# A two-layer fp32 encoder on one core: exchanges issued by GpSimd, later rotary steps, an output projection in two parts, and a last chunk finished block by block

## The chip, the cores and the metric

The kernel runs on one core of one Trainium2 chip. The metric is the device time of one execution in microseconds (us). Three runs of the kernel before gave 2165.27, 2164.92 and 2161.17 us, median 2164.92. The engines are TensorE (PE, matrix multiplications; PEld is its weight load), VectorE (DVE), ScalarE (ACT), GpSimd (POOL) and SyncE (SP, which computes nothing and issues DMAs).

## The reference, cut to what matters

```python
for l in range(2):                                   # 256 tokens, D = 2048, float32
    h = rms(x, ln1_g[l]);  proj = h @ w_in[l]         # 12 column groups: A, B and C heads
    # A: 4 heads, low-rank q and kv, q = rms(a_cq) @ w_uq, kv = rms(a_ckv) @ w_ukv, rotary on 64 columns
    # B: 6 query heads, 2 kv heads, RMSNorm on q and k, 2-D axial rotary
    # C: 6 heads, rotary, mixture of three dilated windows weighted by their log-sum-exp
    mixed = concat([rms(o_a), rms(o_b), rms(o_c)]) * g_out[l]
    x = x + mixed @ w_out[l]                          # output projection, 2048 x 2048
    u = square(relu(rms(x, ln2_g[l]) @ w_ff1[l]))     # 2048 x 8192
    x = x + u @ w_ff2[l]                              # 8192 x 2048
return rms(x, ln_f_g)
```

## The kernel before

Every product is an emulated fp32 one. A weight chunk of 1024 columns (`raw`) is copied by ACT into a rounded part `hi` (L157), and DVE forms `lo = raw - hi` (L158); activations are split in the same way, and TensorE multiplies hi by hi, hi by lo and lo by hi. All weights of the two layers stream once from HBM through three `raw` tiles of 2048 columns, loaded by SP (L142), into five chunk buffers of `hi` and `lo`.

The work is a list of units (L50 to L62), one per weight tile: s0 to s3 and a4 to a7 (low-rank inputs), b0 to b7 with un, ur, uk, uv between (A's and B's queries and keys), v0 to v7 (values), c0 to c11 (two units for each head of C), o0 to o9, w0 to w5 and p0 to p7 (output projection), then f0 to f63 and g0 to g63 (MLP, in four rounds of 16 f and 16 g). A unit of o or w is one chunk of 1024 columns with 12 matmuls; the others are two chunks. A loop (L1042 to L1053) runs a slot for each unit: its matmuls, the functions scheduled at "pre", one split of a chunk, "mid", splits up to five chunks ahead, "post", the eviction of the unit, and "ext". What is scheduled where is written with `at(unit, place, function, offset in units)`; each engine executes its instructions in the order of this program.

A projected pair of q and k (tile `z`, evicted from PSUM by L263) needs its partition halves exchanged for the rotary step: `swap` (L337 to L342) copies them by DMA into `zs`, four DMAs of 64 KB for the B group and two of 128 KB for C. SP issues them (L340, L341), in one queue with the weight loads. `rope` (L348) then multiplies both tiles, L355 adds them, and L360 and L361 split the result into the ring tiles of the score matmuls. The heads table (L837) says for each head in which unit the scores (`s_mm`) stand, two units later the transposes, three later the product with the values (`pv_mm`, L737 to L739).

The output projection's 16 k-tiles are the 4 of A, the 6 of B and the 6 of C. Units o0 to o9 do the ten tiles of A and B for column chunks 0 and 1, w0 to w5 C's six for the same chunks, and p0 to p7 all sixteen for chunks 2 and 3; `add_out` (L877) adds a chunk to the residual stream `xt` and takes its squares. f0 (L922) is special: after its first ten k-tiles come the transposes of chunk 3 of the new residual (L278), whose operands (L201 on ACT, L202 on DVE) its own last k-tiles read. The end (L1056 to L1065) starts when the last g unit is done for both blocks of 128 tokens: squares, their mean, a power on GpSimd (L232), then scaling and storing of both blocks.

## Time and profile before

| what | value |
|---|---|
| median of three runs | 2164.92 us |
| the profiled execution: time | 2162.03 us |
| the profiled execution: span of the trace | 2160.0 us |
| busy share of PE, DVE, ACT, POOL | 99%, 63%, 48%, 4% |
| HBM traffic over the span | 183 GB/s |
| DMA queue of SP and ACT | 53.2% of 16 engines' span |
| exchanges: DMAs of 64 KB and 128 KB | 40 and 24 |

Times in the trace count from the start of the span. A row of the timeline gives start and duration, the engine, the program line and the tiles, and in brackets how long the engine had stood idle before it and whose work ended that. A busy share is a mean over the whole span: TensorE is nearly always busy, so the rows to look for are the few at which it stands still, and the stretches in which its granted clock is lower.

### The profile page before, as it was taken

What the parts mean: (1) busy time and instruction counts of PE and PEld (TensorE: products, weight loads), DVE (VectorE), ACT (ScalarE), POOL (GpSimd) and SP (SyncE); (2) the same over time, 40 slices, a digit from 0 to 9 for tenths busy, and PEclk for the clock granted to TensorE, in tenths of its full rate; (3) what the DMA queues carried; (4) which work ended last, traced back from release to release, by engine and by line L of the source; (5) the groups of instructions that cost most, each with busy time, mean ns of one, the idle gap of its engine ahead of it and who ended that gap; (6) DMA issues with size and microseconds to landing.
All of it is one profiled execution on the core that took longest, in us unless ns stands there. A gap on an engine that the chain in (4) does not pass through costs nothing.

```text
span 2160.0 us, 27992 instructions
## 1 busy us (share of the span) xinstructions
PE 2132.9 (99%) x11132; PEld 1825.8 (85%) x11132; DVE 1367.7 (63%) x1867; ACT 1037.8 (48%) x1549; POOL 90.8 (4%) x108
## 2 busy tenths in 40 slices
PE   9999999999999999999999999999999999999997
PEld 8888878888888888888888888788888888888886
DVE  7787865665564565566577778656646655655654
ACT  7555554543453444344454565545434434534443
POOL 2001110000000000000020011100000000000000
PEclk9999999999999999999999999999999999999999
DMA  8644454555555555555554544545655555565563
GB/s 303 202 154 147 151 193 163 195 195 201 174 206 199 175 190 203 177 191 191 199 185 166 170 149 154 196 159 195 211 195 176 199 194 175 193 214 176 187 223 117
DMA packets 64018, 401.90 MB, mean 186 GB/s; under 512 B 7824, under 2 KB 7824, under 8 KB 19216
## 3 DMA queue, kind: packets, MB, share of 16 engines
q1 hardware_dynamic: 61440, 394.29, 53.2%
q10 hardware_dynamic: 2448, 5.83, 0.8%
q8 instruction: 87, 1.43, 0.3%
q14 instruction: 43, 0.35, 0.0%
HBM read 392.23 MB, written 2.10 MB: 183 GB/s over the span
## 4 chain that ended last, share of the span: by engine, by line
PE 56%; issue 37%; DVE 3%; ACT 2%; DMA 1%; POOL 0%; SPq 0%; POOLq 0%; DVEq 0%; ACTq 0%
PE acc L307 16%; PE acc L639 8%; PE acc L641 8%; PE acc L640 8%; PE acc L308 8%; PE acc L416 1%; PE att L307 1%; DMA z<-z 1%; DVE lo L158 1%; PE att L737 1%; ACT hi L157 1%; PE acc L417 1%; DVE z L348 1%; PE att L738 1%; PE att L739 1%
## 5 line engine op out<-in xcount | busy, mean ns | idle before, releaser
L158 DVE TENSOR_TENSOR lo<-raw,hi 128x1024 fp32r<-128x1024 f32 (+1 forms) x735 | 883.2, 1228 | 377.9 <-ACT hi L157 373.5
L307 PE MATMUL acc<-hx,hi 128*128 128x512 f32 x2720 | 950.4, 394 | 1.7 <-ACT hi L157 1.7
L157 ACT ACTIVATE hi<-raw 128x1024 fp32r<-128x1024 f32 (+1 forms) x735 | 752.7, 1051 | 380.1 <-PE acc L641 348.0
L308 PE MATMUL acc<-hx,lo 128*128 128x256 f32 x2720 | 761.6, 280 | 1.5 <-DVE lo L158 1.5
L307 PEld LDWEIGHTS acc<-hx,hi 128*128 128x128 f32 x2720 | 512.5, 188 | 114.9 <-ACT hi L157 2.4
L308 PEld LDWEIGHTS acc<-hx,lo 128*128 128x128 f32 x2720 | 511.8, 188 | 2.4 <-DVE lo L158 2.1
L639 PE MATMUL acc<-hi,ring 128*128 128x512 f32 x1296 | 506.7, 391 | 0.0
L641 PE MATMUL acc<-hi,ring 128*128 128x512 f32 x1296 | 504.8, 389 | 0.0
L640 PE MATMUL acc<-lo,ring 128*128 128x512 f32 x1296 | 504.7, 389 | 0.0
L641 PEld LDWEIGHTS acc<-hi,ring 128*128 128x128 f32 x1296 | 243.5, 188 | 51.0
L639 PEld LDWEIGHTS acc<-hi,ring 128*128 128x128 f32 x1296 | 243.6, 188 | 50.0
L640 PEld LDWEIGHTS acc<-lo,ring 128*128 128x128 f32 x1296 | 243.7, 188 | 49.7
L262 ACT ACTIVATE t<-acc 128x256 f32<-128x256 f32 x192 | 73.4, 384 | 310.1 <-PE acc L308 304.3
L263 DVE TENSOR_TENSOR t<-acc,t 128x256 f32<-128x256 f32 x140 | 59.1, 424 | 123.2 <-ACT t L262 123.2
L943 ACT ACTIVATE ring<-t 128x256 fp32r<-128x256 f32 x128 | 53.5, 418 | 126.0 <-DVE t L941 126.0
L972 DVE SCALAR_TENSOR_TENSOR xt<-acc,st,xt 128x512 f32<-128x512 f32 x64 | 45.8, 751 | 86.2 <-PE acc L641 86.2
L944 DVE TENSOR_TENSOR ring<-t,ring 128x256 fp32r<-128x256 f32 x128 | 54.4, 425 | 62.6 <-ACT ring L943 62.6
L267 ACT ACTIVATE sq<-xt 128x512 f32<-128x512 f32 x40 | 25.1, 629 | 71.7 <-DVE xt L972 44.0
L941 DVE SCALAR_TENSOR_TENSOR t<-t 128x256 f32<-128x256 f32 x128 | 54.4, 425 | 4.4
L639 PE MATMUL acc<-hi,hx 128*128 128x512 f32 x128 | 50.9, 398 | 0.0
L640 PE MATMUL acc<-lo,hx 128*128 128x512 f32 x128 | 50.0, 391 | 0.0
L641 PE MATMUL acc<-hi,hx 128*128 128x512 f32 x128 | 49.9, 390 | 0.0
(152 smaller groups left out, 1273.5 us busy)
## 6 DMA issues: line engine op xcount, KB each, us to landing
raw<-in_w_dram SPq DMA_DIRECT2D x347, 1024.0 KB, 4.9
raw<-in_w_dram SPq DMA_DIRECT2D x39, 512.0 KB, 3.7
z<-z SPq DMA_DIRECT2D x24, 128.0 KB, 3.7
z<-z SPq DMA_DIRECT2D x40, 64.0 KB, 4.2
ring<-in_xfeat_dram SPq DMA_DIRECT2D x8, 256.0 KB, 7.5
ring<-in_tabs_dram ACTq DMA_DIRECT2D x8, 256.0 KB, 4.6
xt<-in_xtok_dram ACTq DMA_DIRECT2D x2, 1024.0 KB, 10.0
ring<-in_gfin_dram ACTq DMA_DIRECT2D x4, 256.0 KB, 4.3
```

The lines of the kernel that those rows point to most:

```text
L157: act.activation(out=hi[:, :n], in_=t, func=AF.Copy)
L158: dve.tensor_tensor(out=lo[:, :n], in0=t, in1=hi[:, :n].bitcast(F32), op=ALU.subtract)
L262: act.activation(out=t, in_=acc[:, T:], func=AF.Copy)
L263: dve.tensor_tensor(out=dst, in0=acc[:, :T], in1=t, op=ALU.add)
L307: pe.matmul(acc, h, s, start=k == 0, stop=False)
L308: pe.matmul(acc[:, T:], lo, s[:, :T], start=False, stop=k == n - 1)
L639: pe.matmul(a, sh, h, start=first, stop=False)
L640: pe.matmul(a, sh, lo, start=False, stop=False)
L641: pe.matmul(a, sl, h, start=False, stop=last)
L941: dve.scalar_tensor_tensor(out=z, in0=z, scalar=0.0, in1=z, op0=ALU.max, op1=ALU.mult)
L943: act.activation(out=d[:, :T], in_=z, func=AF.Copy)
L944: dve.tensor_tensor(out=d[:, T:], in0=z, in1=d[:, :T].bitcast(F32), op=ALU.subtract)
```

## The change

- The exchanges of `swap` are issued from GpSimd's queue and no longer from SP's.
- The first weight unit is split into four chunks of 512 columns, and its second half is loaded as two DMAs.
- B's rotary multiplication (`b_rope`) moves from "post" of its u unit to "pre" of the unit after it; the last C head's rotary step moves one more unit back, and C's last three heads get their transposes and value products one or two units later.
- o0 to o19 now do A's and B's ten k-tiles for all four column chunks, w0 to w11 C's six; the p units are gone. Each chunk is added to the residual twice; its squares are taken at the second time. C's group sum moves from o6 to o9.
- f0 does its first 12 k-tiles and then the transposes of chunk 3; f1 does its own first 12, then the last four of f0 and of itself. Both are evicted in f1's slot.
- In the last layer the last two g units run all of block 0 first and then all of block 1, and `last_chunk` finishes and stores each block by itself.

```diff
--- before
+++ after
...
 def split_chunks(u, n):
     if u == 0:
-        return [512, 512, 1024]
+        return [512] * 4
     return [n] if n <= 1024 else [n // 2, n // 2]
...
     names += [f"c{m}" for m in range(12)]
-    names += [f"o{m}" for m in range(10)]
-    names += [f"w{m}" for m in range(6)]
-    names += [f"p{m}" for m in range(8)]
+    names += [f"o{m}" for m in range(20)]
+    names += [f"w{m}" for m in range(12)]
     for q in range(4):
...
     xf = [ring() for _ in range(8)]
-    parts = [(0, 0, 512), (0, 512, 1024), (0, 1024, 2048), (1, 0, 1024), (1, 1024, 2048), (2, 0, 1024),
-             (2, 1024, 2048)]
+    parts = [(0, 0, 512), (0, 512, 1024), (0, 1024, 1536), (0, 1536, 2048), (1, 0, 1024), (1, 1024, 2048),
+             (2, 0, 1024), (2, 1024, 2048)]
     for g in range(8):
         sp.dma_start(out=xf[g], in_=xfeat[g])
-        if g == 0:
-            load_part(*parts.pop(0))
-        if parts:
-            load_part(*parts.pop(0))
+        for _ in range(2 if g < 2 else 1):
+            if parts:
+                load_part(*parts.pop(0))
     loaded[0] = RAW_BUFS
...
             for a in range(0, P, 2 * w):
-                sp.dma_start(out=zs[a:a + w], in_=z[a + w:a + 2 * w])
-                sp.dma_start(out=zs[a + w:a + 2 * w], in_=z[a:a + w])
+                pool.dma_start(out=zs[a:a + w], in_=z[a + w:a + 2 * w])
+                pool.dma_start(out=zs[a + w:a + 2 * w], in_=z[a:a + w])
             return z, zs
...
             at(name, "pre", b_sq)
-            at(name, "post", lambda p=p: b_rope(p))
+            at(name, "pre", lambda p=p: b_rope(p), 1)
             at(name, "pre", lambda p=p: b_rope2(p), 2)
...
-        def v_mm(name, srcs, k0, kt, accs=None, n=4):
-            for k in range(n):
+        def v_mm(name, srcs, k0, kt, accs=None, n=4, blocks=(0, 1)):
+            for k, tb in [(k, tb) for k in range(n) for tb in blocks]:
                 h, lo = wtile(base + POS[name], k, 512)
...
                 first, last = k0 + k == 0, k0 + k == kt - 1
...
+                a = (accs or st["accv"])[tb]
+                sh = s[:, tb * P:(tb + 1) * P]
+                sl = s[:, T + tb * P:T + (tb + 1) * P]
+                pe.matmul(a, sh, h, start=first, stop=False)
+                pe.matmul(a, sh, lo, start=False, stop=False)
+                pe.matmul(a, sl, h, start=False, stop=last)
...
         for h in range(6):
-            d = 1 if h == 5 else 0
+            d = 2 if h == 5 else 0
             at(POS["c0"] + 2 * h + 2 + d, "pre" if d else "post", lambda h=h: c_rope(h))
...
-        heads = [("A", h, POS["b7"] + h) for h in range(4)]
-        heads += [("B", h, POS["v2"] + h) for h in range(6)]
-        heads += [("C", h, POS["c3"] + 2 * h + (h == 5)) for h in range(6)]
-        for (g, h, s) in heads:
+        heads = [("A", h, POS["b7"] + h, 2, 3) for h in range(4)]
+        heads += [("B", h, POS["v2"] + h, 2, 3) for h in range(6)]
+        heads += [("C", h, POS["c3"] + 2 * h, 2, 3) for h in range(3)]
+        heads += [("C", 3, POS["c9"], 2, 4), ("C", 4, POS["c11"], 3, 5), ("C", 5, POS["o3"], 3, 5)]
+        for (g, h, s, dt, dp) in heads:
             hs = {}
-            at(s + 3, "ext", lambda g=g, h=h, hs=hs: pv_mm(g, h, hs))
-            at(s + 2, "ext", lambda hs=hs: transp(hs))
+            at(s + dp, "ext", lambda g=g, h=h, hs=hs: pv_mm(g, h, hs))
+            at(s + dt, "ext", lambda hs=hs: transp(hs))
             at(s, "ext", lambda g=g, h=h, hs=hs: s_mm(g, h, hs))
-            at(s + 4, "pre", lambda g=g, h=h, hs=hs: o_ev(g, h, hs))
-            at(s + 3, "pre", lambda hs=hs: t_copy(hs))
+            at(s + dp + 1, "pre", lambda g=g, h=h, hs=hs: o_ev(g, h, hs))
+            at(s + dt + 1, "pre", lambda hs=hs: t_copy(hs))
             at(s + 1, "pre", lambda g=g, h=h, hs=hs: s_max(g, h, hs))
...
-        for (g, name, n, k0, per) in (("A", "v5", 4, 0, 2), ("B", "c3", 6, 4, 2), ("C", "o6", 6, 10, 3)):
+        for (g, name, n, k0, per) in (("A", "v5", 4, 0, 2), ("B", "c3", 6, 4, 2), ("C", "o9", 6, 10, 1)):
             s = POS[name]
...
             at(s + 1, "pre", lambda g=g, n=n: grp_fin(g, n * P))
-            d = 1 if g == "B" else 0
+            d = 0 if g == "A" else 1
             at(s + 1 + d, "pre" if d else "post", diag("r" + g))
...
-        def add_out(accs, c):
+        def add_out(accs, c, whole):
             for tb in range(2):
                 dve.tensor_tensor(out=xc(tb, c), in0=accs[tb], in1=xc(tb, c), op=ALU.add)
-            for tb in range(2):
-                square_sum(st2["ssx"], tb, c)
+            if whole:
+                for tb in range(2):
+                    square_sum(st2["ssx"], tb, c)
...
+        def mk_o(name, c, j, k0, n):
             def f():
...
                     st["acco", c] = [accbank(), accbank()]
...
+                mixed = [st["mixed"].get(k0 + k) for k in range(2 * n)]
+                v_mm(name, mixed, 2 * j, 2 * n, st["acco", c], 2)
+            define(name, f, lambda: add_out(st["acco", c], c, k0 > 0) if j == n - 1 else None)
+            if k0 and j == n - 1 and c < 3:
+                turn(name, 1, c)
+        for i in range(20):
+            mk_o(f"o{i}", i // 5, i % 5, 0, 5)
+        for i in range(12):
+            mk_o(f"w{i}", i // 3, i % 3, 10, 3)
...
+            def part(i, ks):
+                if ks[0] == 0:
+                    st2["acc", i] = accbank()
+                acc = st2["acc", i]
+                for k in ks:
+                    h, lo = wtile(base + POS[f"f{i}"], k)
+                    s = st2["hx"][k]
+                    pe.matmul(acc, h, s, start=k == 0, stop=False)
+                    pe.matmul(acc[:, T:], lo, s[:, :T], start=False, stop=k == KT - 1)
             def f():
                 if i == 0:
...
+                    part(0, range(12))
+                    st2["turn"] = x_transposes(3)
+                elif i == 1:
+                    part(1, range(12))
+                    part(0, range(12, KT))
+                    part(1, range(12, KT))
+                else:
+                    st2["acc", m] = gemm_acc(f"f{i}", 0, st2["hx"])
+            def evict():
+                if i == 1:
+                    ev(0)
+                if i:
+                    ev(m)
+            def ev(m):
                 acc = st2.pop(("acc", m))
...
+        at("f0", "post", lambda: x_operands(3, st2["turn"], st2, G_LN2, l))
         at("f2", "post", r2_fin)
...
                     st["accg"] = [accbank(), accbank()]
+                if l + 1 == DEPTH and i >= 62:
+                    v_mm(f"g{i}", st2["u"], 4 * j, 16, st["accg"], blocks=(0,))
+                    if i == 63:
+                        for d in (1, 0):
+                            v_mm(f"g{i - d}", st2["u"], 4 * (j - d), 16, st["accg"], blocks=(1,))
+                    return
                 v_mm(f"g{i}", st2["u"], 4 * j, 16, st["accg"])
...
                 if j < 3:
+                    return
+                if i == 63 and l + 1 == DEPTH:
+                    last_chunk(st["accg"], st["r2sq"])
                     return
...
             at("g48", "post", load_gfin)
+            at("g62", "post", first_means)
...
             dve.tensor_tensor(out=xc(tb, c), in0=xc(tb, c), in1=gf[c], op=ALU.mult)
+    def first_means():
+        for tb in range(2):
+            t = stat(2)
+            dve.tensor_reduce(out=t[:, 0:1], in_=final_state["ssx"][:, 4 * tb:4 * tb + 3], axis=AX.X, op=ALU.add)
+            dve.tensor_scalar(out=t[:, 1:2], in0=t[:, 0:1], scalar1=1.0 / D, scalar2=EPS, op0=ALU.mult, op1=ALU.add)
+            final_state["mean", tb] = t[:, 1:2]
+    def last_chunk(accs, scale):
+        ss = final_state["ssx"]
+        y = [ring() for _ in range(2)]
+        for tb in range(2):
+            dve.scalar_tensor_tensor(out=xc(tb, 3), in0=accs[tb], scalar=scale[:, tb:tb + 1], in1=xc(tb, 3),
+                                     op0=ALU.mult, op1=ALU.add)
+            square_sum(ss, tb, 3)
+            dve.tensor_tensor(out=y[tb], in0=xc(tb, 3), in1=gf[3], op=ALU.mult)
+            ms, r = stat(2), stat(2)
+            dve.tensor_scalar(out=ms[:, 0:1], in0=ss[:, 4 * tb + 3:4 * tb + 4], scalar1=1.0 / D,
+                              scalar2=final_state["mean", tb], op0=ALU.mult, op1=ALU.add)
+            pool.tensor_tensor(out=r[:, 0:1], in0=ms[:, 0:1], in1=nhalf[:, 0:1], op=ALU.pow)
+            dve.tensor_scalar(out=xt[tb][:, :1024], in0=xt[tb][:, :1024], scalar1=r[:, 0:1], scalar2=None, op0=ALU.mult)
+            act.activation(out=y[tb], in_=y[tb], func=AF.Copy, scale=r[:, 0:1])
+            dve.tensor_scalar(out=xc(tb, 2), in0=xc(tb, 2), scalar1=r[:, 0:1], scalar2=None, op0=ALU.mult)
+            sp.dma_start(out=out[tb][:, :1024], in_=xt[tb][:, :1024])
+            act.dma_start(out=out[tb][:, 1536:], in_=y[tb])
+            sp.dma_start(out=out[tb][:, 1024:1536], in_=xc(tb, 2))
...
     assert not sched
...
```

The order of the instructions shows three places. Names: `raw`, `hi`, `lo` are a weight tile and its parts, `z` on the right of a DMA is the pair and on the left its copy, `st` small statistics, `acc` PSUM accumulators, `hx` activation operands.

Before, SP's queue in the first head group of layer 1, exchanges between weight loads:

```order
L341 DMA z_204_972<-z_193_917 32x512
L142 DMA raw_1005<-in_w_dram 128x2048
L142 DMA raw_1104<-in_w_dram 128x2048
L340 DMA z_227_1106<-z_213_1009 32x512
L341 DMA z_227_1106<-z_213_1009 32x512
```

After, GpSimd's queue at the same place, between the power of the low-rank norms (L487) and the next one (L554), with the end of one exchange and the start of the next:

```order
L487 TENSOR_TENSOR st_753<-st_752,nhalf 128x4
...
L336 DMA z_206_977<-z_195_922 32x512
L337 DMA z_206_977<-z_195_922 32x512
L336 DMA z_229_1111<-z_215_1012 32x512
L337 DMA z_229_1111<-z_215_1012 32x512
...
L554 TENSOR_TENSOR st_1441<-st_1440,nhalf 128x16
```

Two weight loads stood between these two exchanges before; now the second directly follows the first, 20 exchange DMAs in a row between the two powers.

Before, VectorE at the end of the third head group (L348 is the rotary multiplication of the last head, L809 the copy of transposed probabilities for which `pv_mm` of the head before it waits in the same unit):

```order
L796 TENSOR_SCALAR p_2981<-p_2981,st_2997 128x256 x2
L158 TENSOR_TENSOR lo_3002<-raw_2937,hi_3001 128x1024
L348 TENSOR_TENSOR z_620_2880<-z_620_2880,ring_1633 128x512
L348 TENSOR_TENSOR z_635_2948<-z_635_2948,ring_1634 128x512
L355 TENSOR_TENSOR z_620_2880<-z_620_2880,z_635_2948 128x512
L158 TENSOR_TENSOR lo_3035<-raw_2943,hi_3034 128x1024
L361 TENSOR_TENSOR ring_3058<-z_620_2880,ring_3057 128x512
L809 TENSOR_TENSOR pt_3062<-att_3040,pt_3061 128x512
L158 TENSOR_TENSOR lo_3066<-raw_2992,hi_3065 128x1024
```

After, the same engine at the same place (L344 and L804 are these two lines):

```order
L791 TENSOR_SCALAR p_2986<-p_2986,st_3002 128x256 x2
L155 TENSOR_TENSOR lo_3007<-raw_2942,hi_3006 128x1024
L155 TENSOR_TENSOR lo_3025<-raw_2948,hi_3024 128x1024
L344 TENSOR_TENSOR z_622_2885<-z_622_2885,ring_1638 128x512
L344 TENSOR_TENSOR z_637_2953<-z_637_2953,ring_1639 128x512
L351 TENSOR_TENSOR z_622_2885<-z_622_2885,z_637_2953 128x512
L155 TENSOR_TENSOR lo_3058<-raw_2997,hi_3057 128x1024
L357 TENSOR_TENSOR ring_3081<-z_622_2885,ring_3080 128x512
L804 TENSOR_TENSOR pt_3085<-att_3063,pt_3084 128x512
L155 TENSOR_TENSOR lo_3089<-raw_3010,hi_3088 128x1024
```

One more split of a weight chunk stands ahead of the rotary step, and the transposed copy is read by a product in the next unit; before, the product stood in the copy's own unit.

Before, TensorE at the transposes of chunk 3 in f0 (the first and the last of eight transposes; hx_3787 is the first operand that they yield, and its row is followed by three more k-tiles like it):

```order
L931 MATMUL acc_3756<-hx_3663,lo_3741 128x256
L278 MATMUL att_3777<-ident,xt_85 128x128
...
L278 MATMUL att_3778<-ident,xt_86 128x128
L930 MATMUL acc_3756<-hx_3666,hi_3740 128x512
L931 MATMUL acc_3756<-hx_3666,lo_3741 128x256
L930 MATMUL acc_3756<-hx_3669,hi_3740 128x512
L931 MATMUL acc_3756<-hx_3669,lo_3741 128x256
L930 MATMUL acc_3756<-hx_3787,hi_3740 128x512
```

After, the same place (acc_3799 is f0, acc_3850 is f1; hx_3838 is the first operand from the transposes; f1's twelve k-tiles stand between):

```order
L912 MATMUL acc_3799<-hx_3768,lo_3732 128x256
L274 MATMUL att_3824<-ident,xt_85 128x128
...
L274 MATMUL att_3825<-ident,xt_86 128x128
L911 MATMUL acc_3850<-hx_3593,hi_3771 128x512
L912 MATMUL acc_3850<-hx_3593,lo_3772 128x256
...
L912 MATMUL acc_3850<-hx_3768,lo_3788 128x256
L911 MATMUL acc_3799<-hx_3838,hi_3731 128x512
L912 MATMUL acc_3799<-hx_3838,lo_3732 128x256
```

Twelve k-tiles of f1, 24 matmuls, now lie between the transposes and the first reader of what they yield; before it was two k-tiles, 4 matmuls.

## Rows read from the trace of the kernel before

**Rows 1.** The page, busy time of each engine: busy us (share of span) xinstructions.

```profile
PE 2132.9 (99%) x11132; PEld 1825.8 (85%) x11132; DVE 1367.7 (63%) x1867; ACT 1037.8 (48%) x1549; POOL 90.8 (4%) x108
```

**Rows 2.** Timeline of the start: start us, us, engine line op [idle before <-releaser].

```profile
5.93 0.63 ACT L157 ACTIVATE hi<-raw 128x512 fp32r<-128x512 f32 x1 [0.60 <-DMA raw<-in_w_dram]
...
6.60 0.69 DVE L158 TENSOR_TENSOR lo<-raw,hi 128x512 fp32r<-128x512 f32 x1 [0.54 <-ACT hi L157]
...
9.22 1.06 ACT L157 ACTIVATE hi<-raw 128x1024 fp32r<-128x1024 f32 x1 [1.24 <-DMA raw<-in_w_dram]
...
10.31 1.23 DVE L158 TENSOR_TENSOR lo<-raw,hi 128x1024 fp32r<-128x1024 f32 x1 [1.81 <-ACT hi L157]
...
11.59 0.39 PE L417 MATMUL acc<-hx,lo 128*128 128x256 f32 x1 [0.76 <-DVE lo L158]
```

**Rows 3.** The same view, layer 1, first head group.

```profile
88.85 9.14 SPq L142 DMA_DIRECT2D raw<-in_w_dram  x2
...
95.46 0.69 DVE L361 TENSOR_TENSOR ring<-z,ring 128x512 fp32r<-128x512 f32 x1 [0.70 <-ACT ring L360]
...
104.50 1.29 DVE L348 TENSOR_TENSOR z<-z,ring 128x512 f32<-128x512 f32 x2 [2.04 <-DMA z<-z]
...
114.91 0.39 PE L308 MATMUL acc<-hx,lo 128*128 128x256 f32 x1 [0.77 <-DVE lo L158]
```

**Rows 4.** The same view, TensorE, the same place in layer 2.

```profile
1186.68 0.50 PE L307 MATMUL acc<-hx,hi 128*128 128x512 f32 x1 [1.66 <-ACT hi L157]
```

**Rows 5.** The same view, TensorE, end of the third head group, layer 1.

```profile
282.18 0.38 PE L737 MATMUL att<-pt,ring 128*128 128x256 f32 x1 [2.87 <-ACT pt L808]
283.37 0.38 PE L738 MATMUL att<-pt,ring 128*128 128x256 f32 x1 [0.81 <-DVE pt L809]
```

**Rows 6.** The same view, TensorE, the same place in layer 2.

```profile
1355.87 0.38 PE L737 MATMUL att<-pt,ring 128*128 128x256 f32 x1 [1.97 <-ACT pt L808]
```

**Rows 7.** The chain that ended last, before that end: start us, us, what.

```profile
272.26 6.67 DMA z<-z
```

**Rows 8.** Stretches: us, busy us (x) by engine, PEclk, DMA share, GB/s.

```profile
283.80:287.30 3.50, 3.50 (x15) 3.11 (x14) 2.17 (x4) 1.60 (x3) 0.74 (x1) 0.51 0.69 241
304.00:370.00 66.00, 66.00 (x305) 54.92 (x304) 39.84 (x48) 33.43 (x52) 4.51 (x6) 1.00 0.56 200
1188.40:1191.80 3.40, 3.40 (x12) 2.92 (x11) 2.76 (x5) 1.09 (x4) 0.00 (x0) 0.50 0.83 289
```

**Rows 9.** The exchanged tiles: duration ns min/median/max, and DMA issue to landing.

```profile
L340 SPq DMA_DIRECT2D z<-z x32: 467/513/613, 67.9 to 1346.3; - x32
...
DMA to landing us min/median/max: 2.0/4.0/6.7
```

**Rows 10.** GpSimd's groups by shape: busy us, mean ns of one, idle before.

```profile
L558 POOL TENSOR_TENSOR st<-st,nhalf 128x16 f32<-128x16 f32 x2 | 5.8, 2910 | 142.2 <-DVE st L557 142.2
...
L491 POOL TENSOR_TENSOR st<-st,nhalf 128x4 f32<-128x4 f32 x2 | 2.0, 1022 | 9.0 <-DVE st L490 9.0
```

**Rows 11.** Timeline of TensorE, first unit of the MLP, layer 1.

```profile
374.55 0.48 PE L930 MATMUL acc<-hx,hi 128*128 128x512 f32 x1
...
378.35 0.39 PE L307 MATMUL acc<-hx,hi 128*128 128x512 f32 x1
```

**Rows 12.** VectorE's additions of the output projection, by shape.

```profile
L879 DVE TENSOR_TENSOR xt<-acc,xt 128x512 f32<-128x512 f32 x16 | 10.6, 688 | 9.8 <-PE acc L641 9.8
```

**Rows 13.** The page's DMA issues: count, KB each, median us from issue to landing.

```profile
raw<-in_w_dram SPq DMA_DIRECT2D x39, 512.0 KB, 3.7
```

**Rows 14.** Timeline of the end.

```profile
2146.75 0.39 PE L640 MATMUL acc<-lo,ring 128*128 128x512 f32 x1
...
2148.33 0.39 PE L641 MATMUL acc<-hi,ring 128*128 128x512 f32 x1
...
2150.80 0.70 POOL L232 TENSOR_TENSOR st<-st,nhalf 128x2 f32<-128x2 f32 x1 [766.22 <-DVE st L231]
...
2154.30 0.96 SPq L1065 DMA_DIRECT2D out_dram<-xt  x1
```

More of the change, by code (lines that the diff above doesn't have):

```diff
@@ L31, in first_columns @@
 def first_columns(name, chunk):
-    if name == "uv" or name[0] in "vowpg":
+    if name == "uv" or name[0] in "vowg":
         return 0, 0
@@ L634, in v_mm @@
                 first, last = k0 + k == 0, k0 + k == kt - 1
-                for tb in range(2):
-                    a = (accs or st["accv"])[tb]
-                    sh = s[:, tb * P:(tb + 1) * P]
-                    sl = s[:, T + tb * P:T + (tb + 1) * P]
-                    pe.matmul(a, sh, h, start=first, stop=False)
-                    pe.matmul(a, sh, lo, start=False, stop=False)
-                    pe.matmul(a, sl, h, start=False, stop=last)
+                a = (accs or st["accv"])[tb]
[4 more added lines that the diff above has]
+                pe.matmul(a, sl, h, start=False, stop=last)
         def v_ev(scale):
@@ L875, in layer @@
         nxt = layer_state[l + 1] if l + 1 < DEPTH else final_state
-        def add_out(accs, c):
+        def add_out(accs, c, whole):
             for tb in range(2):
                 dve.tensor_tensor(out=xc(tb, c), in0=accs[tb], in1=xc(tb, c), op=ALU.add)
-            for tb in range(2):
-                square_sum(st2["ssx"], tb, c)
+            if whole:
+                for tb in range(2):
+                    square_sum(st2["ssx"], tb, c)
         def turn(name, d, c):
@@ L922, in f @@
             def f():
                 if i == 0:
-                    acc = st2["acc", m] = accbank()
-                    for k in range(KT):
-                        if k == 10:
-                            x_operands(3, x_transposes(3), st2, G_LN2, l)
-                        h, lo = wtile(base + POS["f0"], k)
-                        s = st2["hx"][k]
-                        pe.matmul(acc, h, s, start=k == 0, stop=False)
-                        pe.matmul(acc[:, T:], lo, s[:, :T], start=False, stop=k == KT - 1)
@@ L945, in ev @@
                 st2["u"].append(d)
-            define(f"f{i}", f, ev)
+            define(f"f{i}", f, evict)
         def r2_fin():
@@ L1054 @@
     assert not sched
-    r = rsqrt_mean(total(final_state["ssx"]), D, 2)
-    for tb in range(2):
-        dve.scalar_tensor_tensor(out=xc(tb, 3), in0=xc(tb, 3), scalar=r[:, tb:tb + 1], in1=gf[3], op0=ALU.mult,
-                                 op1=ALU.mult)
-        act.activation(out=xt[tb][:, :512], in_=xt[tb][:, :512], func=AF.Copy, scale=r[:, tb:tb + 1])
-        dve.tensor_scalar(out=xt[tb][:, 512:1536], in0=xt[tb][:, 512:1536], scalar1=r[:, tb:tb + 1], scalar2=None,
-                          op0=ALU.mult)
-        sp.dma_start(out=out[tb][:, 1536:], in_=xc(tb, 3))
-        act.dma_start(out=out[tb][:, :512], in_=xc(tb, 0))
-        sp.dma_start(out=out[tb][:, 512:1536], in_=xt[tb][:, 512:1536])
 def _tables():
@@ L1156, in _weights @@
                 put(rows(wo, (5 + i % 3) * 256, i // 3, 2))
-            elif kind == "p":
-                put(rows(wo, i % 4 * 512, 2 + i // 4, 4))
             elif kind == "f":
```

26 lines of the change are left out of this document (1 added, 25 removed).

## The prediction

> **What bounds the kernel now.** I read the page's busy times first: TensorE works 2132.9 of the 2160.0 us of the span [rows 1]. The change adds no matmul and takes none away (the same products in another order), so what it can give back lies in the few places where TensorE stands still or has a lower granted clock, and behind its last matmul. I looked for these in the timeline of TensorE, then asked for the waits there, and followed the chain that ended last into each. There are five. (1) At the start TensorE waits for the first chunk of 1024 columns: its copy takes 1.06 us and its subtraction 1.23, where the 512-column chunks before it took 0.63 and 0.69 [rows 2]. (2) In the first head group VectorE stands 2.04 us before a rotary multiplication, because the exchange came late: SP's queue was taken by two weight loads from 88.85 to 97.99 [rows 3]. The split behind it then comes late to TensorE, by 0.77 in layer 1 [rows 3] and, at the same place in layer 2, by 1.66 [rows 4] and once more by the step that costs 0.77 in layer 1; there follows a stretch of 3.4 us in which the granted clock is 0.50, the 1.2 GHz level [rows 8]. (3) At the end of the third group TensorE stands for 2.87 and 0.81 us [rows 5], with 3.5 us at 0.51 behind it [rows 8], and for 1.97 in layer 2 with the second step again [rows 6]; the chain shows the cause, an exchange that took 6.67 us to land while VectorE held everything behind its rotary step [rows 7]. (4) In f0 six k-tiles take from 374.55 to 378.35 [rows 11]. (5) The end, from the last matmul's start at 2148.33 to 2160.0 [rows 14].
>
> **The change part by part.** All sums are on the profiled execution: 2162.03 us, its span of 2160.0 and 2.0 around it.
>
> *Start.* Splitting the 1024-column chunk in halves takes 0.43 off the copy and 0.54 off the subtraction that TensorE waits for [rows 2], 0.97 together; the half also lands sooner than the whole. I take 1.2. Bounds: 0, if the second half then arrives just as late, and 2.2, if the idle 1.24 us of ScalarE before the copy [rows 2] went as well.
>
> *Exchanges from GpSimd.* 64 DMAs leave SP's queue, 20 per layer in the first group. No row shows what GpSimd needs to issue one. From below: 0.47, SP's shortest [rows 9]; from above: 2.91, GpSimd's dearest instruction [rows 10]. I take 1.0, by the power on four columns (1.02), an instruction of that engine with almost no data [rows 10]. From issue to landing the rows give 2.0 to 6.7, median 4.0 [rows 9]; I take 2.5, near the short end, because the queue holds no loads. For the exchange of rows 3 the buffer is free at 96.15, when L361 ends; four issues and the landing give 96.15 + 4.0 + 2.5 = 102.65, against 102.46, when VectorE was free before its wait (104.50 less 2.04). So the wait of 2.04 shrinks to some 0.2, and b_rope is later by the move to the next unit besides. The weight loads gain too: none stands behind an exchange that waits for its pair. That frees 0.77 + 1.66 + 0.77 of standing and half of 3.4 us, 1.7, of clock: 4.9. Bounds: −26 (the second rival) and 6.0, since the slow first matmuls after each stop come back as well.
>
> What a page says against it: the Trainium skill, "DMA: Bandwidth & Descriptors", section "Issuing engines are not separate DMA queues", has it that DMAs of whichever engine share the same 16 DMA engines and interleave, and that another issuer only saves issue time. No run here shows it for GpSimd; by that rule the landing would stay at its median. What this is worth is the first rival.
>
> *Third group.* The last head's rotary step stands one unit later, and the product of the head before no longer shares its unit with the copy that it reads. A unit of o is 12 matmuls; seven steps take 2148.33 − 2146.75 = 1.58, so 0.226 each and 2.71 a unit [rows 14]. The exchange landed at 278.93 [rows 7], and TensorE then lost 2.87 + 0.81 = 3.7. Of that 2.71 is given back by the later rotary step alone, even if the landing stays at 6.67, and the unit between copy and product is as much again. So this term hardly hangs on the new queue. It gives 2.87 + 0.81 + 1.97 + 0.81 and half of 3.5, 1.7: 8.2. From above I allow 9.2, for the slow first matmuls after each stop, and from below 3, if VectorE, which has these heads beside a split of 1.23 in every unit of 2.71, hands the wait on to the next product.
>
> *Output projection.* 16 additions more, at 0.688 us 11.0 in all [rows 12], in a region in which VectorE is busy 39.8 of 66 us [rows 8]: nothing. Without that cover each eviction would hold a pair of accumulators 1.4 us longer. The weights come in 64 loads of 512 KB where there were 32 and 16 of 1 MB, and three tiles in flight then hold half as much: a tile's cycle is landing 3.7 [rows 13] + copy 1.06 + subtraction 1.23 [rows 2] = 6.0, over three tiles 2.0 per unit, against TensorE's 2.71. Nothing, as long as landing stays under 3 × 2.71 − 2.29 = 5.8. C's group sum moves with C's heads and is read by the w units only, several units of o later; nothing.
>
> *f0 and f1.* Six k-tiles in 3.80 us [rows 11]; at two matmuls of 512 and 256 columns, 0.226 + half of it, they need 6 × 0.34 = 2.0. The excess, about 1.7 per layer, goes, since 24 matmuls (12 × 0.34 = 4.1 us) now stand between the transposes and their reader, and before the change these operands were all read by 378.35, so they take less than 3.8. I take 3.0 for both layers, a little under 3.4, since f1 has the eviction of two units behind it.
>
> *End.* The power is done at 2151.50, 3.2 after the last matmul's start [rows 14]; about the same comes out with one block left (one eviction and one square less, beside work that ran in parallel): −0.2. Scaling both blocks took until 2154.30, 2.8; one block takes about 1.15 (its 1024 columns, then 512, at half of 2.8 less what ScalarE does), −1.65. From the last issue's end (2155.26) to the end are 4.7 us, in which the output drains; half of it now leaves under the 24 matmuls of block 1 (24 × 0.226 = 5.4 us). I take a quarter of 4.7 for that, 1.2; bounds 0 and 2.4. Together 3.1, 1.9 to 4.3.
>
> *Sum.* 1.2 + 4.9 + 8.2 + 3.0 + 3.1 = 20.4, so 2162.03 − 20.4 = 2141.6 for an execution like the profiled one. That execution is 2.9 below the median shown and the three runs spread over 4.1, so I add a third of the difference: 2142.5.
>
> **Rivals.** *Landing stays* (chance 0.20). The exchanges meet the weight loads on the DMA engines whoever issues them, and landing stays at 4.0 or goes to 6.7. For it: the 6.67 of rows 7 followed an issue without delay. Then 96.15 + 4.0 + 4.0 = 104.15, as late as before (104.50): term 2 gives nothing, and C's heads, which have a shorter way to their rotary step, lose part of what term 3 gives, some 2: 2142.5 + 4.9 + 2 = 2149.
>
> *GpSimd is slow to issue* (0.07, the slower side). At 2.91 per DMA the exchange of rows 3 is there at 96.15 + 11.6 + 2.5 = 110.3, 7.8 after VectorE needs it, and the next one, directly behind it in the same queue, another 11.6 later with about 6 us of VectorE's work between: 13 per layer and 26 in all, as every split stands behind these steps on VectorE. With term 2 lost: 2142.5 + 4.9 + 26 = 2173. At 1.0 the cost is 0, so a microsecond per DMA costs 26 / 1.9 = 13.6; it turns slower than before from 1.0 + (2164.9 − 2147.4) / 13.6 = 2.3 on. Against it: SP's issue is 0.47 to 0.61, and GpSimd's instruction with little data 1.0.
>
> A page that bears on this: the Trainium skill, "SBUF — State Buffer", section "SBUF: two separate sides", says that a DMA from GpSimd's queue can't have its descriptors written while VectorE runs an operation that holds both ports, a two-port one such as a plain fp32 copy, and counts an operation with two SBUF inputs only against GpSimd's reads. By it, a subtraction of 1.23 us holds nothing up; were it read as holding every operation with two inputs, the issue would wait for most of VectorE's time, and the slower side of this rival is what it gives. No row of before shows a DMA of GpSimd.
>
> *Weight supply* (0.08). If the landing of a 512 KB load goes from 3.7 to 6.0 or more because four queues and twice as many loads interleave, the cycle is (6.0 + 2.29) / 3 = 2.76, over 2.71; at 6.67 it is 2.99, 0.28 for each of 64 units, 18 us: 2160. In between, about 2152.
>
> *The waits only move* (0.05). Third-group waits go to the product two units on, or f1 stops where f0 did; all but the start and the end stays: 2162 − 4.3 + 0.9 = 2159, near no change.
>
> **How the numbers follow.** The forecast has 0.60 and goes from 2135 (every term at its upper bound, 2.2 + 6.0 + 9.2 + 3.4 + 4.3 = 25, off 2162.03 gives 2137, and 2 for the spread of the runs) to 2147 (the third group at its lower bound). The range for 8 in 10 reaches on to the first rival and part of the third: 2135 to 2155. About 0.2% (4.3 us) is what a measurement of this kernel can tell from no change, so faster is below 2160.6: the forecast, the first rival and most of the third, with a part of the fourth, 0.88; slower, above 2169.2, only the second rival, 0.06; the rest, 0.06, is the same.
>
> **What would show it.** In the profile after: GpSimd's DMA issues near 1 us each; VectorE's idle time before the rotary multiplication under 5 us in all; no stop of TensorE over 0.5 us at the five places but the start; no stretch at the lower clock level in the head groups; 8.5 us from the last matmul's start to the end; and loads of 512 KB that land in under 5 us. It is wrong if TensorE stops before split chunks in the o and w units (weight supply), if VectorE waits longer for exchanges than before (slow issue), or if GpSimd's issue rows are over 2 us.

## The result and the profile after

The changed kernel takes 2145.73 us (median of four runs, 2143.04 to 2147.7) against 2163.53 of the kernel before (four runs): ratio 0.9918, 95% interval 0.9900 to 0.9935. The forecast was 2142.5, in a range of 2135 to 2155. The profiled execution took 2143.04 us with a span of 2141.3; before it was 2162.03 and 2160.0. It is the fastest of the four, and the forecast lies under all of them: the median fell by 17.8 us, where 22.4 were forecast (2164.92 to 2142.5).

Both programs run 11132 matmuls, and outside the units that the change reorders these stand in the same sequence. So the start of the matmul with the same number can be compared. This table gives the time from one such mark to the next, worked out from the starts in the two traces (the rows below show its last marks):

| stretch, up to the start of | before | after | difference |
|---|---|---|---|
| the 73rd matmul (start) | 17.08 | 17.30 | +0.23 |
| a6 | 25.18 | 25.18 | 0 |
| uv (first group), layers 1 and 2 | 77.42, 80.59 | 76.06, 76.06 | −1.36, −4.53 |
| o0 (from uv over the v and c units), layers 1 and 2 | 150.00, 150.01 | 150.00, 149.97 | 0, −0.04 |
| f0 (the o and w units: end of the third group, projection), layers 1 and 2 | 100.58, 98.09 | 96.10, 95.42 | −4.49, −2.67 |
| g0 (first MLP units), layers 1 and 2 | 91.29, 91.29 | 89.72, 89.72 | −1.57, −1.57 |
| all other g, f, s and a units | | | 0 |
| the end, behind the last matmul's start | 11.69 | 8.93 | −2.75 |

The differences add up to −18.8, the change of the span. The waits that the prediction named are gone from the list of TensorE's waits (engine, line, waited for: us in all, times, longest), and of the five places two are left:

```profile
PE att L733 <- DVE ring L357: 2.3, 4, 0.7
PE small L165 <- POOL ones L162: 1.0, 1, 1.0
PE acc L413 <- DVE lo L155: 1.0, 2, 0.8
```

The first row is the scores of the third group: the fourth head's, 1.0 us in two times as before, and now the last head's. The second is the matmuls that warm up the engine, which the kernel before had too, and the last is the start. For the exchanges [rows 9] now reads, in the same view:

```profile
L336 POOL DMA_DIRECT2D z<-z x32: 496/497/697, 68.5 to 1334.8; - x32
...
  DMA z<-z: 4.3, 5
...
DMA to landing us min/median/max: 1.8/2.9/5.7
```

GpSimd issues a DMA in 0.50 us, no slower than SP (0.51, [rows 9]); the landing's median fell from 4.0 to 2.9, and VectorE waits 4.3 us in all for exchanges; the page's group of 64 KB exchanges went from 4.2 to 2.7. At the place of [rows 3] GpSimd and VectorE now show (timeline):

```profile
95.11 0.50 POOL L336 DMA_DIRECT2D z<-z  x1 [7.88 <-DVE z L351]
...
96.57 0.50 POOL L337 DMA_DIRECT2D z<-z  x1
```

```profile
95.52 0.69 DVE L357 TENSOR_TENSOR ring<-z,ring 128x512 fp32r<-128x512 f32 x1 [0.70 <-ACT ring L356]
...
102.61 1.29 DVE L344 TENSOR_TENSOR z<-z,ring 128x512 f32<-128x512 f32 x2
```

The first issue starts at 95.11, when VectorE's addition has released the buffer (even sooner than the prediction had it), where SP came to it at 98 or later; the rotary multiplication has no wait. In the stretch of f0 and f1 [rows 11], up to the readers of what the transposes yield, TensorE has no gap (stretch, us, busy us of PE, PEld, VectorE, ScalarE and GpSimd, granted clock, DMA share, GB/s):

```profile
364.00:378.00 14.00, 14.00 (x84) 12.35 (x83) 9.82 (x14) 8.06 (x15) 0.00 (x0) 1.00 0.41 138
```

The end [rows 14] in the timeline, one block left:

```profile
2132.32 0.39 PE L636 MATMUL acc<-hi,ring 128*128 128x512 f32 x1
...
2134.58 0.55 POOL L1030 TENSOR_TENSOR st<-st,nhalf 128x1 f32<-128x1 f32 x1 [4.76 <-DVE st L1028]
...
2136.38 0.38 SPq L1036 DMA_DIRECT2D out_dram<-xt  x1
```

And the third group's end [rows 5, 6], where a smaller stop stands at another matmul, the last head's scores:

```profile
281.20 0.38 PE L732 MATMUL att<-ring 128*128 128x256 f32 x1 [0.39 <-ACT ring L356]
282.27 0.39 PE L733 MATMUL att<-ring,ring 128*128 128x256 f32 x1 [0.69 <-DVE ring L357]
```

### The profile page after: what moved, and what is told of

It reads as the page before. It is cut to its first block, busy times and chain, and to the rows that moved or that the text cites. A ratio compares the mean times of both kernels' runs of the same rounds, so it can differ in the third digit from the quotient of the medians.

```text
span 2141.3 us, 28079 instructions
## 1 busy us (share of the span) xinstructions
PE 2127.8 (99%) x11132; PEld 1825.1 (85%) x11132; DVE 1378.3 (64%) x1890; ACT 1036.4 (48%) x1550; POOL 125.6 (6%) x173
## 3 DMA queue, kind: packets, MB, share of 16 engines
q0 software_dynamic: 2432, 5.77, 1.1%
## 4 chain that ended last, share of the span: by engine, by line
PE 94%; DVE 2%; ACT 2%; issue 1%; DMA 1%; SPq 0%; POOLq 0%; POOL 0%; DVEq 0%; ACTq 0%
PE acc L303 27%; PE acc L634 15%; PE acc L636 15%; PE acc L635 15%; PE acc L304 14%; PE acc L412 1%; PE att L303 1%; PE att L732 1%; PE acc L911 1%; ACT hi L154 1%; PE att L733 1%; PE acc L413 1%; PE att L734 1%; DVE lo L155 1%; PE att L304 1%
## 5 line engine op out<-in xcount | busy, mean ns | idle before, releaser
L303 PE MATMUL acc<-hx,hi 128*128 128x512 f32 x2688 | 937.4, 393 | 0.0
L304 PE MATMUL acc<-hx,lo 128*128 128x256 f32 x2688 | 753.2, 280 | 0.0
L303 PEld LDWEIGHTS acc<-hx,hi 128*128 128x128 f32 x2688 | 506.6, 188 | 111.1
L304 PEld LDWEIGHTS acc<-hx,lo 128*128 128x128 f32 x2688 | 505.6, 188 | 0.2
L263 ACT ACTIVATE sq<-xt 128x512 f32<-128x512 f32 x40 | 25.1, 627 | 62.2 <-DVE xt L978 31.4
L634 PE MATMUL acc<-hi,hx 128*128 128x512 f32 x128 | 50.9, 398 | 0.0
## 6 DMA issues: line engine op xcount, KB each, us to landing
xt<-in_xtok_dram ACTq DMA_DIRECT2D x2, 1024.0 KB, 10.4
```

The costliest lines, as they stand in the source:

```text
L303: pe.matmul(acc, h, s, start=k == 0, stop=False)
L304: pe.matmul(acc[:, T:], lo, s[:, :T], start=False, stop=k == n - 1)
L634: pe.matmul(a, sh, h, start=first, stop=False)
```

## The experiments

The theory: the first group's waits are those of a queue that exchanges share with weight loads; the third group's are those of a reader that stands in the unit of the step that makes its operand. The rivals are given with each run. Times with one run are single runs; the marks of the table above tell the stretches apart to 0.1 us.

**Exchanges back on SP (x_sp)**

```diff
-                pool.dma_start(out=zs[a:a + w], in_=z[a + w:a + 2 * w])
-                pool.dma_start(out=zs[a + w:a + 2 * w], in_=z[a:a + w])
+                sp.dma_start(out=zs[a:a + w], in_=z[a + w:a + 2 * w])
+                sp.dma_start(out=zs[a + w:a + 2 * w], in_=z[a:a + w])
```

> The changed kernel with one edit undone: the exchanges are issued from SP's queue again; the later rotary step stays. Theory (the queue): the waits of the first head group come back, VectorE stands over 12 us in all before rotary multiplications (4.3 in the changed kernel, 17.4 in the one before), TensorE stops again before late splits, and the span goes from 2141.3 to 2145 to 2147 us. Rival (the place): the later rotary step alone took these waits away, and the span stays within 1 us of 2141.3.

Measured: span 2147.1. The first group takes 77.39 and 77.41 us (76.06 with GpSimd's queue), so its gain is gone in layer 1 and falls from 4.53 to 3.19 in layer 2. VectorE waits 10.4 us for exchanges, a little under the 12 expected. At 104.94 it waits as it did at 104.50:

```profile
104.94 1.29 DVE L344 TENSOR_TENSOR z<-z,ring 128x512 f32<-128x512 f32 x2 [2.01 <-DMA z<-z]
```

TensorE's stop follows as before, 0.76 at 115.36. Another 1.56 is lost in layer 1's v units, where TensorE never stands still but has a stretch at the lower level of its clock, 13.5 us behind that stop; before, the same stretch ran at full clock:

```profile
128.90:132.40 3.50, 3.50 (x9) 2.75 (x9) 2.75 (x9) 0.00 (x0) 0.74 (x1) 0.51 0.65 256
```

So SP's queue brings the waits back, and for layer 1 it is the cause. In layer 2 the stop of 1.66 [rows 4] does not return with it: there the later rotary step alone is enough in this profile.

**The rotary step back in its own unit (x_rope)**

```diff
-            at(name, "pre", lambda p=p: b_rope(p), 1)
+            at(name, "post", lambda p=p: b_rope(p))
```

> The changed kernel with B's rotary multiplication back at the end of its own unit; the exchanges stay on GpSimd's queue. Theory (the queue): the span stays within 1.5 us of 2141.3, with a longer wait of VectorE for one exchange but none of TensorE. Rival (the place): the first group's waits come back and the span is 2145 to 2147 us.

Measured: span 2145.7, which looks like the rival, but the stretches say otherwise: the first group takes 76.06 us in both layers, exactly as after. VectorE's wait for exchanges doubles to 8.8 us and costs TensorE nothing. The 4.4 us more are 0.75 at the start and 2.0 and 1.7 in the projection, where the program is the same; that the changed kernel varies there I come back to. The queue alone gives the whole gain, and the move of this step is worth nothing as long as the queue is GpSimd's.

**A dearer issue (x_slow4, x_slow16)**, a power on GpSimd ahead of each exchange DMA:

```diff
+                pool.tensor_tensor(out=slow_t[:, :4], in0=ones[:, :4], in1=nhalf[:, :4], op=ALU.pow)
                 pool.dma_start(out=zs[a:a + w], in_=z[a + w:a + 2 * w])
```

> The changed kernel with a power on 128x4 on GpSimd (1.02 us) ahead of each exchange DMA, so that an issue costs about 1.5 instead of 0.50. It adds work that the result does not use. By the prediction's price (13.6 us for each microsecond over 1.0): 7 us more, 2148. Rival (split chunks prepared ahead and the unit between the exchange and its reader cover it): VectorE waits longer for exchanges, 8 to 15 us in all, but the span stays within 2 us of 2141.3 plus what the projection's units vary.

> The same with a power on 128x16 (2.9 us) ahead of each exchange DMA: an issue costs about 3.4. It adds work that the result does not use. By the prediction's price: 33 us more, 2174, slower than the kernel before. Rival (cover): TensorE stops only in the first group, 3 to 8 us per layer, and the span is 2148 to 2160.

Measured: spans 2160.0 and 2244.0. With the small power the eight DMAs of two exchanges took from 100.22 to 114.29, 1.76 us each:

```profile
100.22 0.56 POOL L338 DMA_DIRECT2D z<-z  x1 [6.07 <-DVE z L354]
...
113.74 0.55 POOL L340 DMA_DIRECT2D z<-z  x1
```

The first group takes 85.39 and 84.59 us, 17.9 more in both layers together, which is 14.2 for each of the 1.26 us over 0.50. VectorE waits 31.4 us for exchanges, and TensorE stops before the product that waits for a split:

```profile
119.58 0.80 PE L304 MATMUL acc<-hx,hi 128*128 128x512 f32 x1 [3.82 <-ACT hi L154]
```

So the chunks split ahead do not cover it, and neither expectation came true: the loss is 18.7 us, and at 1.76 per issue nothing of the change is left. With the large power (3.47 per issue) the first group takes 103.11 and 104.00 us, 55.0 more than after, and the third group loses 33 and the v units and the projection the rest of 102.7. For the first group alone the price in the prediction (13.6 us for each microsecond over 1.0) gives 10 and 34, so it was too low. Where the cost begins these runs don't tell: counted from 0.50, the small power costs 14.2 per microsecond, but from the small power to the large it is 21.7, and a straight line through these two begins near 0.94. A part of the 17.9 is clock, too: in three stretches of the first group, 13.6 us in all, the granted clock is 0.50.

**The third group's old places (x_heads)**

```diff
-            d = 2 if h == 5 else 0
+            d = 1 if h == 5 else 0
...
-        heads += [("C", h, POS["c3"] + 2 * h, 2, 3) for h in range(3)]
-        heads += [("C", 3, POS["c9"], 2, 4), ("C", 4, POS["c11"], 3, 5), ("C", 5, POS["o3"], 3, 5)]
+        heads += [("C", h, POS["c3"] + 2 * h + (h == 5), 2, 3) for h in range(6)]
```

> The changed kernel with the third group's old places: the last head's rotary step one unit earlier, transposes two and value products three units after the scores for all six heads. Exchanges from GpSimd and the output projection in 20 + 12 units stay. Theory (the places): TensorE stops again at the product after a late transposed copy, about 3 us in each layer, and loses clock behind it: 2146 to 2150 us. Rival (the queue): the exchange now lands in time, so the old places cost nothing: within 1 us of 2141.3.

Measured: span 2149.0. o0 to f0 takes 99.15 and 99.90 us, 3.1 and 4.5 more than after, though the exchanges land as fast. The run undoes the three moves of places together and does not tell them apart. The stops are those of before, at the product behind its own copy:

```profile
279.93 0.38 PE L732 MATMUL att<-pt,ring 128*128 128x256 f32 x1 [1.67 <-ACT pt L803]
281.12 0.39 PE L733 MATMUL att<-pt,ring 128*128 128x256 f32 x1 [0.81 <-DVE pt L804]
```

**The old start (x_start)**

```diff
-        return [512] * 4
+        return [512, 512, 1024]
...
-    parts = [(0, 0, 512), (0, 512, 1024), (0, 1024, 1536), (0, 1536, 2048), (1, 0, 1024), (1, 1024, 2048),
+    parts = [(0, 0, 512), (0, 512, 1024), (0, 1024, 2048), (1, 0, 1024), (1, 1024, 2048), (2, 0, 1024),
```

> The changed kernel with the old start: first unit in chunks of 512, 512 and 1024 and its second half in one load. The first unit and the 16 matmuls behind it ended at 17.08 us before, and at 17.30 to 18.05 in the five profiles with the new start. Theory (the first microseconds go by the arrival of activations and weights and by ScalarE's order, and finer pieces only move the wait to the second unit's first chunk): 17.0 to 17.6, no later than with the new start. Rival (the finer pieces help, and the one profile of before was lucky): over 18.

Measured: the 73rd matmul starts at 18.57, later than in any of the profiles with the new start (17.14 to 18.05 in twelve) and than in the one of before with the old (17.08). The number is the rival's, but what made it is the clock. TensorE stands before the third quarter as it did before (there 1.41 and 0.76 us), and behind these stops the granted clock is 0.50 from 11.26 on, where it stayed at full speed before:

```profile
10.53 0.50 PE L413 MATMUL acc<-hx,hi 128*128 128x512 f32 x1 [1.69 <-ACT hi L154]
11.79 0.58 PE L414 MATMUL acc<-hx,lo 128*128 128x256 f32 x1 [0.76 <-DVE lo L155]
```

```profile
11.30:14.60 3.30, 2.81 (x9) 2.42 (x10) 2.46 (x5) 2.28 (x4) 0.00 (x0) 0.50 1.02 358
```

Against before, the matmuls are 0.2 us late at the third quarter and 1.5 at the end of this stretch. At full clock, in the one profile of before, the old start is as fast as the new one (17.08 is under all twelve). The new one has no stop over 0.8 us there and no such stretch in twelve profiles; that it is safer for this reason is a guess from two profiles of the old.

**The changed kernel once more (x_same)**

> The changed kernel itself, unchanged, on the same chip as the next two, to see what its time varies by. All theories: 2143 to 2148 us; the units from the projection to the MLP (o0 to f0) take 95.4 to 99 us, as they did in the profiles with the same program there, and every other stretch behind the first units the same within 0.1 us.

Measured: 2146.61 us (2143.37 to 2147.33, five runs), span 2145.5, 4.3 over the profile of after: 0.5 at the start, and o0 to f0 takes 96.26 and 98.98 us, against 96.10 and 95.42. That stretch is what varies.

**Six half tiles for the raw weights (x_half)**

```diff
-        if c0 == 0:
-            raw_t[u] = sb.tile([P, 2048], F32, tag="raw", name=nm("raw"), bufs=RAW_BUFS)
+        if c0 % 1024 == 0:
+            raw_t[u, c0 // 1024] = sb.tile([P, 1024], F32, tag="raw", name=nm("raw"), bufs=2 * RAW_BUFS)
```

> The changed kernel with the three raw weight tiles of 2048 columns cut into six of 1024, each loaded by its own DMA: the same memory, but a unit of the projection (1024 columns) now has six tiles in flight instead of three. Theory (weight supply: the stop at the last head's scores, 1.6 and 0.9 us in the profile of the changed kernel and up to 4.8 in others, comes from a load that lands 5.4 to 6.6 us after its tile came free, so that copy, subtraction and the rotary step behind it on VectorE are late): o0 to f0 takes 95.3 to 96.0 us in both layers, and the median is 1 to 4 us under that of the changed kernel on the same chip. Rival (the order on VectorE and the addition on GpSimd beside it): the stop stays, o0 to f0 96 to 99 us, no difference in time.

Measured: 2148.53 us (2147.32 to 2149.23), slower than x_same on the same chip. The projection of layer 2 does take 95.05 us, but layer 1 takes 96.15, and the third group's units, 79.1 before, take 80.5 and 83.3: with twice as many loads of half the size in flight the exchanges of the third group land later, and TensorE stops at the scores. Landing after the change was 2.9 at the median; here:

```profile
  DMA z<-z: 17.0, 11
...
DMA to landing us min/median/max: 1.9/5.1/6.5
```

**Later scores (x_late, x_late2, x_late3)**. All three put the scores of C's fourth and last head one unit later; the fourth head's product stands one, two and three units behind its transposes:

```diff
-        heads += [("C", 3, POS["c9"], 2, 4), ("C", 4, POS["c11"], 3, 5), ("C", 5, POS["o3"], 3, 5)]
+        heads += [("C", 3, POS["c10"], 2, 5), ("C", 4, POS["c11"], 3, 5), ("C", 5, POS["o4"], 3, 5)]
```

(the third; the others have 2, 3 and 2, 4 for the fourth head; the group's sum goes from o9 to o10).

> The changed kernel with the scores of the third group's fourth and last head one unit later (and the group's sum one unit later). In the changed kernel TensorE waits at these scores for VectorE's second half of the operand, 0.86 us at the fourth head and 1.6 or 0.9 at the last, in each layer, 4.2 us in all. Theory (order on VectorE, a unit of slack is enough): these four stops go and the span is 2137 to 2138 us, the ratio to the kernel before about 0.9897. Rival (the work of VectorE in these units is the limit): the stops go on to the next reader and the span is 2140 to 2142.

Measured: 2150.52 us (ratio 0.9945, 0.9927 to 0.9963). The stops at the scores are gone, but I had put the fourth head's product into the unit of its copy, and it stops for 2.67 and 1.00 there:

```profile
276.81 0.39 PE L732 MATMUL att<-pt,ring 128*128 128x256 f32 x1 [2.67 <-ACT pt L803]
```

> As the run with later scores, but the fourth head's product stands one unit later too, so that a unit lies between the copy of the transposed probabilities and the product that reads it. In that run the stop at the scores went at both heads (0.95 and 1.25 us less in the third group's units), and a new one of 3 to 4 us stood at the fourth head's product, whose operand is copied in the same unit. Theory (a product or a score must stand one unit behind the step that makes its operand, since VectorE runs up to a unit late): all stops of the third group and behind it go, the projection's units fall by 4.5 to 6 us in layer 1 and 3.5 to 4 in layer 2 against the kernel before, and the span is 2136 to 2137.5 us, ratio about 0.9895. Rival (VectorE's work in these units is the limit and a stop returns elsewhere): 2140 or more.

Measured: 2142.21 us (2141.27 to 2143.07; ratio 0.9907, 0.9892 to 0.9921), span 2140.4. The span misses the 2136 to 2137.5 expected and lies where the rival had it. Layer 2 is as expected (1.25 and 2.76 less than before in c0 to o0 and o0 to f0), layer 1 keeps a stop of 1.00 at that product.

> As the second run with later scores (fourth and last head's scores one unit later, full raw tiles), with the fourth head's product another unit later. In that run one stop of 1.3 us was left, at this product in layer 1, where its operand's copy on VectorE ended while TensorE already waited. Theory (VectorE is a unit and more behind here, and slack in units is what removes a stop): the stop goes, third group and projection together (c0 to f0) take 173.2 to 174 us in both layers, median 2140 to 2142 us, under every run of the changed kernel so far (2143.04 to 2147.7). Rival (any new order makes another stop): c0 to f0 at 175 or more in a layer, median 2143 or more.

Measured: 2140.32 us (2140.26 to 2140.43, four runs), ratio 0.9895, 0.9878 to 0.9911. c0 to f0 takes 173.64 and 172.88 us (175.24 and 174.54 after). Of all waits behind the start this is left:

```profile
283.84 0.38 PE L733 MATMUL att<-pt,ring 128*128 128x256 f32 x1 [0.51 <-DVE pt L804]
```

It lies under all nine runs of the changed kernel (2143.04 to 2147.7), though these were on other chips, and its four runs differ by 0.2 us where those differ by 4: with the stops the variation goes too.

**Both (x_best)**, half tiles with the second arrangement of the scores.

> Six half tiles together with the later scores of the fourth and the last head. If both reasons hold: the units of the third group take 77.9 to 78.2 us instead of 79.1, o0 to f0 95.3 to 95.6, the span is 2137 to 2138.5 us and the ratio to the kernel before 0.9885 to 0.990. If weight supply was the only reason, as the run with half tiles; if it was no reason, as the second run with later scores, 2142 us.

Measured: 2149.91 us (2148.35 to 2151.05). The late exchanges of the half tiles outweigh the rest: the third group takes 82.5 us in layer 1, with a stop of 3 us at scores.

## Why the prediction was right, point by point

*Start*: forecast 1.2 less, measured 0.23 more. This step failed. The third quarter's matmuls did start earlier (9.15 instead of 10.33), but the second unit's first chunk was then late instead:

```profile
13.37 0.50 PE L412 MATMUL acc<-hx,hi 128*128 128x512 f32 x1 [0.22 <-ACT hi L154]
14.63 0.39 PE L413 MATMUL acc<-hx,lo 128*128 128x256 f32 x1 [0.76 <-DVE lo L155]
```

The chain that ended last leads from there to an activation load, issued at 4.49 and landed 6.96 later, which ScalarE waits for ahead of that chunk. The prediction had asked what the wait costs, not what is late next.

*Exchanges*: 4.9 forecast, 5.9 measured, at the bound of 6.0. x_rope shows that the queue alone does it; x_sp, that the move alone keeps 3.19 of it, all in layer 2. The two guesses were off in opposite ways, issue 0.50 instead of 1.0 and landing 2.9 instead of 2.5.

*Third group and projection*: 8.2 forecast, 7.2 measured (4.49, 2.67 and 0.04). The old stops went, as x_heads shows by their return, but at the last head's scores, which the prediction does not name, TensorE now stands 1.5 us beyond its pace in layer 1 and 0.8 in layer 2 in the profile of after, and up to 2.8 in x_start. So the prediction's sign, no stop over 0.5 us but at the start, did not hold (0.69), and its last rival, that waits only move, is true in part. The chain there runs from a weight load through copy, subtraction and rotary step:

```profile
270.23 5.35 DMA raw<-in_w_dram
...
275.68 1.07 ACT hi L154
...
277.92 1.85 DVE z L344 x2
...
281.62 0.61 DVE ring L357
```

The stop follows this load. In layer 2 of x_same, x_rope and x_start the load at this place is

```profile
1334.85 6.09 DMA raw<-in_w_dram
```

```profile
1336.97 6.37 DMA raw<-in_w_dram
```

```profile
1335.62 6.63 DMA raw<-in_w_dram
```

and the stop is 2.3, 2.5 and 2.8 us; in layer 1 of x_sp they are 5.93 and 2.1. In all of them, and in the chain above, the stop is the load less 3.8 to 3.9 us, and where the load is not in the chain (after, layer 2), 0.8 is left. So a part of the rival on weight supply is true: the median landing stayed at 3.7 and no split was late for TensorE's weights, but single loads at the seam to the small tiles are late for what stands behind them on VectorE. That is also what varies most between profiles of the changed kernel: the prediction counted what goes away and had no term for what stands there next. x_half, which was to prove it, doesn't settle it, since it delays the exchanges as well; that more slack removes the stop and the variation, x_late3 shows.

*Additions, 64 small loads*: nothing, as forecast; no stretch shows them but for the load in the chain above, which is one of the small ones (512 KB) and over the 5 us that the prediction allowed.

*f0 and f1*: 3.0 forecast, 3.14 measured. *End*: 3.1 forecast, 2.75 measured. The power ends 2.81 behind the last matmul's start instead of 3.17, so 0.36 (forecast 0.2); from there to the last issue it is 1.25 instead of 2.80, so 1.55 (1.65); and from the last issue's start to the end 4.88 instead of 5.70, so 0.82 (1.2).

*Rivals*: The landing did not stay; the Trainium skill, "DMA: Bandwidth & Descriptors", section "Issuing engines are not separate DMA queues", says that DMAs from all engines interleave on the same DMA engines, and x_half agrees: from the same queue the landing is 5.1 when more loads are in flight. What went away in after was the time behind loads in SP's queue and a part of the landing (4.2 at the median in x_sp), so issue time was not all that was saved. The slow issue didn't happen, but x_slow4 shows that the change had less room than the prediction gave it: at 1.76 per issue the kernel is level with the one before, where the prediction put that at 2.3.

## What to carry to other kernels

A queue that holds loads waiting for buffers delays every small transfer behind it; give the small ones a queue of their own, and measure the issue price there, as 1.26 us more per DMA cost here what the whole change gained. The exchanges changed the kind of their queue as well: the page of after lists 2432 packets under q0 software_dynamic, which the page of before does not have. No run put them on a second queue of SP's kind, such as ScalarE's, so that any queue of their own would do is not shown. Where an in-order engine runs up to a unit late, a reader belongs at least one unit behind the step that makes its operand, and one was not always enough (1.00 us in x_late2, gone with two in x_late3); each reader that was moved closer, or left close, became the next stop. Compare profiles at matmuls with the same number: it shows 0.1 us in a place where run times vary by 4.

## What was not expected of the hardware

With GpSimd's addition beside it, VectorE's rotary multiplication took 1.23 us instead of 0.69, and the addition 1.17 instead of 0.74 (medians of the groups); this happened once in each layer:

```profile
277.44 1.17 POOL L829 TENSOR_TENSOR sacc<-sacc,sq 128x256 f32<-128x256 f32 x1 [5.56 <-ACT sq L828]
```

```profile
277.92 1.84 DVE L344 TENSOR_TENSOR z<-z,ring 128x512 f32<-128x512 f32 x2
```

The Trainium skill, "SBUF — State Buffer", section "SBUF: two separate sides", says that an operation of VectorE with two SBUF inputs and one of GpSimd that reads SBUF exclude each other; these two rows agree. GpSimd's DMA issue, 0.50 at the median and 0.70 at most, shows no such blocking.

The granted clock fell to 0.50, the 1.2 GHz level, behind the stop at the scores of layer 2 in x_same:

```profile
1349.00:1352.20 3.20, 3.20 (x9) 2.46 (x9) 3.10 (x7) 1.10 (x4) 0.00 (x0) 0.50 0.78 239
```

TensorE had stood there for 2.3 us beside the pace of its matmuls; in the profile of after, where it stood for 0.8 at this place, it stayed at full clock. The length of a stop does not decide it alone: in x_rope the clock fell behind one of 1.9 us in layer 1 and not behind one of 2.5 in layer 2, and in the kernel before not behind the stop of [rows 6]; in x_sp it fell 13.5 us behind one of 0.76. What decides is left open.
